# A two-block network on one core: the second mixer's modulation in runs of three pieces, two of its four vectors computed between experts and attention

## The chip, the cores and the metric

The kernel runs on one core of one Trainium2 chip. TensorE (PE) multiplies, VectorE (DVE) and ScalarE (ACT) work on whole tiles, GpSimd (POOL) and SyncE (SP) mostly issue transfers, ScalarE some too. The metric is the device time of one execution in microseconds. Times inside an execution are counted from the start of its profiled span.

## The reference

Two blocks follow one another on 256 tokens of width 1024. The first has two layers (l = 0 and 1), each a hybrid mixer and a gated feed-forward network. The second has two layers as well: a pooling mixer with 16 experts, then attention over the tokens and a context with 16 experts. The second block is modulated: six vectors of 1024 numbers for each of its layers come from a conditioning vector and scale, shift and gate what the layer does.

```python
def adaln(cvec, w_mod, b_mod):
    m = jax.nn.silu(cvec) @ w_mod + b_mod          # w_mod: 1024 x 6144
    m = m.reshape(cvec.shape[:-1] + (6, 1, D_MODEL))
    return tuple(m[..., k, :, :] for k in range(6))

for i in range(DEPTH):                              # second block
    sh1, sc1, g1, sh2, sc2, g2 = adaln(c, w_mod[i], b_mod[i])
    a_lat = modulate(x, norm1_g[i], sh1, sc1)       # rmsnorm * (1 + scale) + shift
    ...
    x = x + g1 * y_lat
    x = x + g2 * hier_moe(modulate(x, norm2_g[i], sh2, sc2), ...)
```

The vectors depend on the conditioning vector alone, so they can be computed at any time before they are used. For layer 1 of the second block they are numbered 0 to 5: shift and scale ahead of the attention (0, 1), the attention's gate (2), shift and scale ahead of the experts (3, 4), the experts' gate (5).

## The kernel before

The matmuls of the first block are exact products in three passes: a weight of 1 MB comes through `load` (line 399) on SP's queue into one of three buffers `stg`, `split` (line 413) makes a high part on ScalarE and a low part on DVE, and `prod` (line 450) issues three matmuls for each block of 128 by 128. The layers of the first block come one after the other (`mixer`, `ffn`), then the second block: `latent` (pooling and the routing of the experts), `experts0` (16 experts, four quads), `attn`, `layer1`.

The modulation is filler for the first block. `adaln` (line 1239) is a generator that is advanced by `fill` (line 597), which `pair` calls after each pair of output blocks and `ffn` between some of its steps; `finish` runs what is left. It handles the vectors that it is given, one after the other. For one vector it takes four 1 MB chunks of `w_mod`. In the first block each chunk comes as two pieces of 512 KB through `load2` (line 408), which issues on POOL's queue into one of three buffers `st2`. A piece is multiplied at line 1267 by four matmuls: 32 columns of the conditioning vectors `sc` are the weights, the piece's 256-column quarters stream, and the four results lie in four groups of 32 partitions of one PSUM bank (`ad`). After eight pieces the bank is copied to `S` (line 1279); at the next vector, four small matmuls at line 1250 turn it into columns and DVE adds the bias into `MV` (line 1251). In the second block `st2` is gone (`st2 = None`, `pools_a`): a chunk comes through `load`, its two halves are two steps of the generator, each chunk has a bank of its own, and its result is copied or added to `S` (lines 1275, 1273).

Which vectors are computed where: layer 0's six in the first mixer, layer 1's vectors 0 to 3 in the second mixer, and 4 and 5 in `latent`, right ahead of the experts.

After the experts a test of the routing's counts (`tc.If`, line 1714) stops the planner from moving instructions across it. Then `attn` (line 1883) issues eight indirect transfers on POOL (`gather`, line 1726), each of 128 rows of 4 KB that the experts wrote to DRAM. `vector_row` and `shift_rows` turn vectors 5 and 3 into rows. `combine` (line 1737) weights the gathered rows by matmuls and adds them to the tokens (`seg` 0) and the context (`seg` 1), `modulate` norms and modulates each, and the projections (`project` and what follows, weights `wqk` through `load`) begin. The list `gate` makes a load wait: one entry is taken for each call of `load`, and where it isn't None, POOL first copies a column of the gathered rows into the buffer (line 404), so the load goes out when the gathers are in. Before, the first two loads of `attn` are free and the third and fourth wait.

The order of instructions on each engine is made by a planner that simulates the program's time: it takes what is ready by the order in which the program names it. `high_priority` moves instructions ahead in that order, and `behind` (line 588) keeps one matmul after another.

Of the kernel before, what the change touches and what calls it, by code (L numbers as in the profile page):

```python
# [8 lines left out]
F32 = mybir.dt.float32  # L9
# [263 lines left out]
class Prog:  # L273
# [925 lines left out]
    def pools_m(self, ctx):  # L1199

        P = self.pools(ctx)
        self.a1 = P("a1m", 4)
        self.pmm = P("pmm3", 3, space=PSUM)
        self.pm1 = P("pm1", 1, space=PSUM)
        self.pmx = P("pmx3", 4, space=PSUM)
        self.wx = P("wx", 3)
        self.b8 = P("b8", 3)
        self.b4 = P("b4", 2)
# [30 lines left out]
    def adaln(self, l, cs):  # L1239

        nc, a = self.nc, self.a
        old = None
        for c in list(cs) + [None]:
            ps = None
            if old is not None:
                o, S = old
                ps = self.bank()
                p2 = ps[:, 256:272].rearrange("p (j n) -> p j n", j=2)
                for j in range(2):
                    nc.tensor.matmul(p2[:, j], S[:, j * 128:j * 128 + 128], self.c["s2"], start=True, stop=True)  # L1250
                nc.vector.tensor_add(self.MV[:, l, 8 * o:8 * o + 8].rearrange("p (g j) c -> p j g c", j=2),
                                     p2.rearrange("p j (g c) -> p j g c", c=2),
                                     self.v(f"bm_{l}", 8 * o, 8).rearrange("p (g j o) -> p j g o", j=2, o=1)
                                     .to_broadcast([128, 2, 4, 2]))
            if c is not None:
                S = self.as_.tile([128, 256], F32, tag="as", name="as")
                for q in range(4):
                    if self.st2 is None:
                        t = self.load(a["w_mod"][l, 4 * c + q])
                        ws = [t[:, :1024], t[:, 1024:]]  # L1260
                    else:
                        ws = [self.load2(a["w_mod"][l, 4 * c + q][:, hf * 1024:hf * 1024 + 1024]) for hf in range(2)]
                    ps = self.bank() if ps is None or self.st2 is None else ps
                    first, last = (0, 1) if self.st2 is None else (-2 * q, 7 - 2 * q)
                    for hf in range(2):
                        for n in range(4):
                            nc.tensor.matmul(ps[32 * n:32 * n + 32, :256], self.sc[:, 2 * q + hf],  # L1267
                                             ws[hf][:, n * 256:n * 256 + 256], start=hf == first, stop=hf == last)
                        if self.st2 is None and hf == 0:
                            yield  # L1270
                    if self.st2 is None:
                        if q:
                            nc.vector.tensor_add(S, S, ps[:, :256])
                        else:
                            nc.scalar.copy(S, ps[:, :256])
                    if q < 3:
                        yield
                if self.st2 is not None:
                    nc.scalar.copy(S, ps[:, :256])
                old = c, S  # L1280
            yield

    def bank(self):
        return self.pad.tile([128, 512], F32, tag="ad", name="ad")

    def mv(self, l, which, seg):
# [596 lines left out]
    def attn(self, x, xc):  # L1883
        nc, a = self.nc, self.a
        hs = []
        R = [self.R[0, 0], self.R[0, 1]]
        G = [self.gather(r) for r in R]

        self.gate += [None] * 2 + [G[1][1][:, 1, :1]] * 2
        self.vector_row(1, 5, 0)  # L1890
        for _ in self.shift_rows(1):
            pass
        for seg, xx in enumerate((x, xc)):
            self.combine(G[seg], R[seg], seg, xx)
            th, tl = self.e8(F32R), self.e8(F32R)

            def sink(kt, t, sh, th=th, tl=tl):
                nc.scalar.activation(th[:, kt], t, AF.Identity, bias=sh)
                nc.vector.scalar_tensor_tensor(tl[:, kt], t, sh, th[:, kt], op0=ALU.add, op1=ALU.subtract)
            self.modulate(xx, 1, "m1_1", 0, seg, sink)  # L1900
            hs.append([(th[:, k], tl[:, k]) for k in range(KT)])
        tabs = {"q": [self.c["cos2"], self.c["sin2"]]}
        t = self.t2()
        tabs["k"] = [t[:, 0], t[:, 1]]
# [18 lines left out]
        for m in range(2):  # L1923
            ps = self.mm()
# [220 lines left out]
    def run(self):  # L2145
        from contextlib import ExitStack
        nc = self.nc
# [7 lines left out]
        with ExitStack() as c1:  # L2155
# [5 lines left out]
            nc.sync.dma_start(x[:, 4:], xT[:, 4:])  # L2161
            nc.sync.dma_start(t[:, 1024:], self.a["w_fm"][0, 0][:, 1024:])
            self.loaded = [t]
            for l, todo in enumerate((chain([None] * 2, self.adaln(0, range(6))), self.adaln(1, range(4)))):
                self.todo = todo
                self.mixer(l, x)
                self.finish()
                if l == 0:
                    self.rows_behind()
                else:  # L2170
                    self.todo = self.context()
                self.ffn(l, x)
                self.finish()
            self.todo = self.adaln(1, range(4, 6))
        self.block2(x, hp)

    def last_stats(self, p):
# [28 lines left out]
```

## Time and profile before

| | us |
|---|---|
| median of three runs | 1724.01 (1720.69 to 1727.6) |
| the profiled execution | 1730.23 |
| its span in the profile | 1728.5 |

| engine | busy us | share of the span |
|---|---|---|
| PE (matmul) | 1650.6 | 95% |
| DVE | 1069.1 | 62% |
| ACT | 807.3 | 47% |
| POOL | 179.9 | 10% |

The page gives each engine's busy time. A busy PE may run at either of its two clock levels; the granted clock of a stretch is a share of the full one. The views used below are a table by stretch, lists of waits, and single instructions in order of time. In these, "x8" behind a group is the count of its records, and a bracket gives the idle time ahead of it and what ended that. A 32-bit matmul of the modulation stands as two records.

### The profile page before, as it was taken

To read this page: it belongs to the slowest core of one execution; us is meant where nothing else is said; L and a number is where in the kernel's file an instruction comes from. 1 tells how busy PE (TensorE), PEld (TensorE's weight loads), DVE (VectorE), ACT (ScalarE), POOL (GpSimd) and SP (SyncE) were. 2 spreads that over 40 slices of the span, in tenths; PEclk is the share of its full clock that TensorE was granted. 3 is DMA by queue.
4 is the path that set the end of the run, shared out by engine and by line. 5 is a ranking of instruction groups with operands and counts; after the bars stand their busy time and mean duration, and the time that the engine had idled before them with its cause. 6 is when DMAs were issued, how large, how long until landed. Compare 5 with 4: busy or idle time off the path is not lost. (4 is left out here: it accounts for less than half of the span.)

```text
span 1728.5 us, 29622 instructions
## 1 busy us (share of the span) xinstructions
PE 1650.6 (95%) x12089; PEld 1407.6 (81%) x12089; DVE 1069.1 (62%) x1946; ACT 807.3 (47%) x1260; POOL 179.9 (10%) x282
## 2 busy tenths in 40 slices
PE   6999999999999999999999999998999799888997
PEld 6977889999999986788999999957777598566453
DVE  5874475666665596367686777467776557555222
ACT  4542264444444373245456554436777634552121
POOL 4211001110000230101011111110000201000000
PEclk9999999999999999999999999988999889998999
DMA  8474157865555666335555648466888734118991
GB/s 332 153 254 156 57 189 252 309 243 189 179 179 187 244 192 221 123 122 208 199 184 171 204 171 270 170 244 229 323 303 302 285 126 123 31 31 316 397 402 55
DMA packets 67212, 359.73 MB, mean 208 GB/s; under 512 B 8040, under 2 KB 13080, under 8 KB 34680
## 3 DMA queue, kind: packets, MB, share of 16 engines
q1 hardware_dynamic: 41280, 279.86, 44.8%
q0 software_dynamic: 25712, 77.81, 13.3%
q8 instruction: 100, 1.64, 0.4%
q14 instruction: 48, 0.39, 0.1%
q10 hardware_dynamic: 72, 0.03, 0.0%
HBM read 339.76 MB, written 14.71 MB: 205 GB/s over the span
## 5 line engine op out<-in xcount | busy, mean ns | idle before, releaser
L424 DVE TENSOR_TENSOR wlo<-stg,whi 128x1024 fp32r<-128x1024 f32 (+1 forms) x379 | 462.3, 1226 | 298.0 <-ACT whi L421 288.2
L421 ACT ACTIVATE whi<-stg 128x1024 fp32r<-128x1024 f32 (+1 forms) x383 | 402.5, 1057 | 482.1 <-PE mm L457 287.6
L456 PE MATMUL mm<-hh,whi 128*128 128x256 f32 x1408 | 409.1, 291 | 9.5 <-ACT hh L462 9.2
L457 PE MATMUL mm<-hl,whi 128*128 128x256 f32 x1408 | 403.5, 287 | 0.7 <-DVE hl L466 0.7
L458 PE MATMUL mm<-hh,wlo 128*128 128x256 f32 x1408 | 402.9, 286 | 0.0
L456 PEld LDWEIGHTS mm<-hh,whi 128*128 128x128 f32 x1408 | 272.9, 194 | 21.6 <-ACT hh L462 9.7
L457 PEld LDWEIGHTS mm<-hl,whi 128*128 128x128 f32 x1408 | 273.0, 194 | 4.2 <-issue 2.8
L458 PEld LDWEIGHTS mm<-hh,wlo 128*128 128x128 f32 x1408 | 272.8, 194 | 2.7 <-issue 2.1
L410 POOL DMA_DIRECT2D st<-in_w_mod x80 | 42.8, 536 | 406.3 <-PE ad L1267 367.8
L493 POOL TENSOR_TENSOR a<-a,a 128x256 f32<-128x256 f32 x30 | 28.0, 935 | 313.2 <-ACT a L491 312.0
L613 PE MATMUL mm<-wlo,hh 128*128 128x512 f32 (+1 forms) x160 | 60.1, 375 | 0.0
L614 PE MATMUL mm<-whi,hl 128*128 128x512 f32 (+1 forms) x160 | 60.0, 375 | 0.0
L612 PE MATMUL mm<-whi,hh 128*128 128x512 f32 (+1 forms) x160 | 59.5, 378 | 0.0
L456 PE MATMUL mm<-lg,whi 128*128 128x256 f32 x192 | 54.5, 284 | 0.0
L456 PE MATMUL mx<-lg,whi 128*128 128x256 f32 x192 | 54.4, 285 | 0.0
L457 PE MATMUL mm<-lg,whi 128*128 128x256 f32 x192 | 54.3, 283 | 0.0
L458 PE MATMUL mm<-lg,wlo 128*128 128x256 f32 x192 | 54.3, 283 | 0.0
L1767 PE MATMUL mm<-Dt,tok 128*128 128x256 f32 x256 | 43.0, 316 | 11.8 <-ACT xg L1769 10.0
L457 PE MATMUL mx<-lg,whi 128*128 128x256 f32 x192 | 54.2, 283 | 0.0
L458 PE MATMUL mx<-lg,wlo 128*128 128x256 f32 x192 | 54.1, 283 | 0.0
L1267 PE MATMUL ad<-st,sc 128*32 128x256 f32 x640 | 52.0, 390 | 2.2 <-DMA st<-in_w_mod 2.0
L1861 DVE TENSOR_TENSOR eo<-mx,g2r 128x512 f32<-128x512 f32 x16 | 11.1, 692 | 66.1 <-PE mx L1856 65.8
(601 smaller groups left out, 3597.8 us busy)
## 6 DMA issues: line engine op xcount, KB each, us to landing
stg<-in_moe SPq DMA_DIRECT2D x57, 1024.0 KB
stg<-in_w_gu SPq DMA_DIRECT2D x44, 1024.0 KB
stg<-in_w_fm SPq DMA_DIRECT2D x43, 1024.0 KB
st<-in_w_mod POOLq DMA_DIRECT2D x80, 512.0 KB, 5.8
w<-in_moe SPq DMA_DIRECT2D x27, 1024.0 KB
stg<-in_w_dn SPq DMA_DIRECT2D x22, 1024.0 KB
stg<-in_w_tm SPq DMA_DIRECT2D x16, 1024.0 KB
stg<-in_w_br SPq DMA_DIRECT2D x12, 1024.0 KB
```

Source lines behind the costliest of these rows:

```text
L410: self.nc.gpsimd.dma_start(t, src)
L421: nc.scalar.activation(hi[:, :n], t, AF.Copy)
L424: (nc.gpsimd if pool else nc.vector).tensor_sub(lo[:, :n], t, hi[:, :n])
L456: nc.tensor.matmul(out, hi, xh, start=first and k == 0, stop=False)
L457: nc.tensor.matmul(out, hi, xl, start=False, stop=False)
L458: nc.tensor.matmul(out, lo, xh, start=False, stop=last and k == n - 1)
L493: self.adder.tensor_add(sq[0][1], sq[0][1], s)
L612: nc.tensor.matmul(ps[i], xh[:, ts], hi[:, s], start=first, stop=False)
L613: nc.tensor.matmul(ps[i], xh[:, ts], lo[:, s], start=False, stop=False)
L614: nc.tensor.matmul(ps[i], xl[:, ts], hi[:, s], start=False, stop=last)
L1267: nc.tensor.matmul(ps[32 * n:32 * n + 32, :256], self.sc[:, 2 * q + hf], ws[hf][:, n * 256:n * 256 + 256], start=hf == first, stop=hf == last)
L1767: nc.tensor.matmul(ps[:, w], tok[seg][w][:, t, k * 128:k * 128 + 128], Dt[seg][:, t].rearrange("p e s -> p (e s)"), start=t == 0, stop=t == 1)
```

## The change

In layer 1, `adaln` takes a new path while `st2` exists: `adaln_runs` loads the eight pieces of a vector in runs of three, three and two, each run a step of the generator. A run's matmuls start with its last piece, and all that follow the first are moved ahead in the planner's order (by 400) and tied one behind another. All eight pieces of a vector add up in one bank, from piece 2 (`start`) to piece 6 (`stop`).

The second mixer computes vectors 0 and 1 alone. `latent` computes 3 and 5 in place of 4 and 5. Vectors 2 and 4 are computed in `attn`: eight steps of the generator after the combine of `seg` 0, eight after that of `seg` 1, the rest before the projections. Their eight 1 MB loads go out on SP's queue ahead of the projections' weights, with no gate; the first two projection loads now wait for the gathers. Their bank is the one that the attention's output uses later (`pmo`).

```diff
--- before.py
+++ after.py
@@ -1203,6 +1203,7 @@
         self.pmm = P("pmm3", 3, space=PSUM)
         self.pm1 = P("pm1", 1, space=PSUM)
         self.pmx = P("pmx3", 4, space=PSUM)
+        self.pad = None
         self.wx = P("wx", 3)
         self.b8 = P("b8", 3)
         self.b4 = P("b4", 2)
@@ -1254,6 +1255,12 @@
                                      .to_broadcast([128, 2, 4, 2]))
             if c is not None:
                 S = self.as_.tile([128, 256], F32, tag="as", name="as")
+                if self.st2 is not None and l:
+                    ps = yield from self.adaln_runs(l, c, ps)
+                    nc.scalar.copy(S, ps[:, :256])
+                    old = c, S
+                    yield
+                    continue
                 for q in range(4):
                     if self.st2 is None:
                         t = self.load(a["w_mod"][l, 4 * c + q])
@@ -1280,7 +1287,30 @@
                 old = c, S
             yield
 
+    def adaln_runs(self, l, c, ps):
+
+        nc = self.nc
+        ps = self.bank() if ps is None else ps
+        for run in ((0, 1, 2), (3, 4, 5), (6, 7)):
+            ws = [(z, self.load2(self.a["w_mod"][l, 4 * c + z // 2][:, (z % 2) * 1024:(z % 2) * 1024 + 1024])) for z in run]
+            ms = [(z, w, n) for z, w in reversed(ws) for n in range(4)]
+
+            def mat(z, w, n):
+                return nc.tensor.matmul(ps[32 * n:32 * n + 32, :256], self.sc[:, z], w[:, n * 256:n * 256 + 256],
+                                        start=z == 2, stop=z == 6)
+            e = mat(*ms[0])
+            with self.tc.high_priority(offset=400):
+                for m in ms[1:]:
+                    f = mat(*m)
+                    self.behind(f, e)
+                    e = f
+            if run[0] != 6:
+                yield
+        return ps
+
     def bank(self):
+        if self.pad is None:
+            return self.pmo.tile([128, 512], F32, tag="su", name="ad")
         return self.pad.tile([128, 512], F32, tag="ad", name="ad")
 
     def mv(self, l, which, seg):
@@ -1886,12 +1916,15 @@
         R = [self.R[0, 0], self.R[0, 1]]
         G = [self.gather(r) for r in R]
 
-        self.gate += [None] * 2 + [G[1][1][:, 1, :1]] * 2
+        self.gate += [None] * 8 + [G[1][1][:, 1, :1]] * 2
         self.vector_row(1, 5, 0)
         for _ in self.shift_rows(1):
             pass
+        self.todo = self.adaln(1, (2, 4))
         for seg, xx in enumerate((x, xc)):
             self.combine(G[seg], R[seg], seg, xx)
+            for _ in range(8):
+                self.fill()
             th, tl = self.e8(F32R), self.e8(F32R)
 
             def sink(kt, t, sh, th=th, tl=tl):
@@ -1899,6 +1932,7 @@
                 nc.vector.scalar_tensor_tensor(tl[:, kt], t, sh, th[:, kt], op0=ALU.add, op1=ALU.subtract)
             self.modulate(xx, 1, "m1_1", 0, seg, sink)
             hs.append([(th[:, k], tl[:, k]) for k in range(KT)])
+        self.finish()
         tabs = {"q": [self.c["cos2"], self.c["sin2"]]}
         t = self.t2()
         tabs["k"] = [t[:, 0], t[:, 1]]
@@ -2161,7 +2195,7 @@
             nc.sync.dma_start(x[:, 4:], xT[:, 4:])
             nc.sync.dma_start(t[:, 1024:], self.a["w_fm"][0, 0][:, 1024:])
             self.loaded = [t]
-            for l, todo in enumerate((chain([None] * 2, self.adaln(0, range(6))), self.adaln(1, range(4)))):
+            for l, todo in enumerate((chain([None] * 2, self.adaln(0, range(6))), self.adaln(1, range(2)))):
                 self.todo = todo
                 self.mixer(l, x)
                 self.finish()
@@ -2171,7 +2205,7 @@
                     self.todo = self.context()
                 self.ffn(l, x)
                 self.finish()
-            self.todo = self.adaln(1, range(4, 6))
+            self.todo = self.adaln(1, (3, 5))
         self.block2(x, hp)
 
     def last_stats(self, p):
```

## Rows read from the trace of the kernel before

**Rows 1.** The page: busy time, share of the span, instructions of PE.

```profile
PE 1650.6 (95%) x12089; PEld 1407.6 (81%) x12089; DVE 1069.1 (62%) x1946; ACT 807.3 (47%) x1260; POOL 179.9 (10%) x282
```

**Rows 2.** Busy time by stretch, second mixer: last three clock, DMA share, GB/s.

```profile
565.00:598.00 33.00, 33.00 (x292) 29.55 (x291) 18.86 (x32) 13.54 (x21) 10.04 (x16) 1.00 0.71 254
640.00:667.00 27.00, 24.86 (x143) 15.34 (x144) 15.45 (x23) 10.58 (x17) 4.77 (x9) 1.00 0.81 286
```

**Rows 3.** Waits of PE, 515 to 815 us: total, times, longest.

```profile
PE ad L1267 <- DMA st<-in_w_mod: 2.0, 1, 2.0
```

**Rows 4.** PE in order of time, experts to attention: start, length, what.

```profile
1374.79 0.56 PE L549 MATMUL mx<-vec,MV 128*2 128x20 f32 x16
1380.36 1.20 PE L1750 MATMUL mx<-b,rows 128*128 128x128 f32 x4 [5.01 <-DMA rows<-eb,si]
...
1383.73 1.91 PE L1750 MATMUL ms<-b,rows 128*128 128x128 f32 x8
...
1389.16 1.06 PE L1750 MATMUL ms<-b,rows 128*128 128x128 f32 x8
...
1406.26 0.36 PE L457 MATMUL mm<-b,whi 128*128 128x256 f32 x1
```

**Rows 5.** Busy time by stretch, experts to attention (columns as in rows 2).

```profile
1375.00:1380.00 5.00, 0.35 (x14) 0.23 (x10) 3.16 (x5) 3.96 (x9) 3.84 (x4) 0.74 1.01 392
1380.00:1385.00 5.00, 3.48 (x14) 3.22 (x15) 2.52 (x3) 1.84 (x3) 0.94 (x1) 0.50 1.03 419
1385.00:1390.00 5.00, 5.00 (x36) 5.00 (x35) 0.00 (x0) 0.00 (x0) 0.89 (x3) 0.74 0.90 284
```

**Rows 6.** The modulation's matmuls, 515 to 815 us: records, min/median/max ns.

```profile
L1267 PE MATMUL ad<-st,sc x250: 379/379/403, 567.7 to 812.9; 128*32 128x256 f32 x125
```

**Rows 7.** PE in order of time, second mixer, around groups of the modulation.

```profile
567.71 1.05 PE L1267 MATMUL ad<-st,sc 128*32 128x256 f32 x10
...
587.45 0.28 PE L458 MATMUL mm<-hh,wlo 128*128 128x256 f32 x1
587.66 1.50 PE L1267 MATMUL ad<-st,sc 128*32 128x256 f32 x24
...
589.31 0.28 PE L457 MATMUL mm<-hl,whi 128*128 128x256 f32 x1
...
594.71 0.28 PE L457 MATMUL mm<-hl,whi 128*128 128x256 f32 x1
594.83 0.28 PE L458 MATMUL mm<-hh,wlo 128*128 128x256 f32 x1
595.04 0.64 PE L1267 MATMUL ad<-st,sc 128*32 128x256 f32 x8
...
595.83 0.28 PE L457 MATMUL mm<-hl,whi 128*128 128x256 f32 x1
...
759.48 0.51 PE L1250 MATMUL ad<-cst_cg,as 128*128 128x8 f32 x4
...
812.24 1.07 PE L1267 MATMUL ad<-st,sc 128*32 128x256 f32 x16
```

**Rows 8.** The modulation's 512 KB loads, line 410: issue to landing.

```profile
DMA to landing us min/median/max: 3.8/5.9/9.8
```

**Rows 9.** SP, POOL and ACT in order of time, experts to attention.

```profile
1367.54 21.28 SPq L405 DMA_DIRECT2D stg<-in_wqk  x4
...
1370.93 1.04 POOL L1732 DMA_INDIRECT rows<-eb,si  x1 [2.91 <-ACT a L528]
...
1379.66 1.06 ACT L421 ACTIVATE whi<-stg 128x1024 fp32r<-128x1024 f32 x1 [1.04 <-issue]
...
1388.28 0.31 POOL L404 COPY stg<-rows 128x1 f32<-128x1 f32 x2 [0.32 <-DMA rows<-eb,si]
```

**Rows 10.** DMA queues (q1 is SP's, q0 POOL's), 1371 to 1377 us: packets, MB.

```profile
q1 hardware_dynamic: 198, 1.37, 55.1%
q0 software_dynamic: 254, 0.98, 44.0%
```

## The prediction

> **What bounds the kernel now.** I read the page's busy shares first, then the stretches, then the waits, then single instructions. TensorE (PE) is busy for 95% of the span [rows 1], but that is a mean, so the two places that the change touches were read by themselves. [...]
>
> The second place is the wait between experts and attention, from 1365 to 1406 us. PE ends its row work at 1375.35, then sits idle for 5.01 us until the first gathered rows land at 1380.36; after that it works on the combine, and the attention's projections run in earnest from 1406.26 [rows 4]. [...]
>
> **The change part by part.** *Modulation left in the second mixer.* Before, it has 4 vectors there, each of 32 matmuls of a 128 by 32 weight block, which the trace counts as 64 records; the trace kept 250 of 256 [rows 6]. Eight records are a piece (512 KB), so there are 32 pieces. What a group costs is read from the starts of its neighbours, which come every 0.12 us where nothing is between them. One piece alone: from L458 at 594.83 to the second matmul after the group at 595.83 are 1.00 us, less two steps of 0.12 leaves 0.76 us [rows 7]. Three pieces in one group: 587.45 to 589.31 are 1.86, less 0.24 leaves 1.62 us [rows 7]. The difference, 0.86 for two pieces, is 0.43 us a piece, and what is left is 0.33 us for each time that PE turns to this shape and back. Reading the timeline from the first group at 567.71 to the last at 812.24 [rows 7], I count 27 groups of 2 to 24 records. Cost before: 27 x 0.33 + 32 x 0.43 = 8.9 + 13.8 = 22.7 us. After: 2 vectors, 16 pieces in 6 runs: 6 x 0.33 + 16 x 0.43 = 2.0 + 6.9 = 8.9 us. That is 13.8 us less. Each vector also has a turn-over into columns, four records of 0.51 us in all [rows 7]; two of them go, 1.0 us. Sum: **14.8 us less**, all on PE where it is full.
>
> *The wait of a run.* A run starts with its last piece, so PE now waits for three loads where it waited for one, six times in all, and every matmul of the projections queued behind it on PE waits too. Before, no run exists, so the price has bounds: below, the one old wait of 2.0 us goes too (-2.0); above, the time from issue to landing, which is 5.9 us in the middle and 9.8 at worst [rows 8], so 3.9 us for each of six runs, 23 us. I take 0, since 32 waits on these loads came to 2.0 us [rows 3] and the first run's loads can be issued long ahead. On POOL's queue a run's three loads wait together for the three buffers; behind them stand the second mixer's compression weights, which use the same buffers, and its small casts. I cost this at nothing: PE did not wait for either before [rows 3].
>
> *Two vectors moved into the wait.* They bring 8 loads of 1 MB on SP's queue, through three buffers, ahead of the first load of the projections' weights; 8 times 16 records; a copy or an add for each load on ScalarE or DVE; and the two turn-overs. PE's part at full clock is 8 x (0.33 + 2 x 0.43) + 1.0 = 10.5 us. Before, two projection loads went ahead of the gathers, and the second had landed by 1379.66, where its split starts [rows 9]. Now three buffers are filled at once, 1.05 MB more ahead of the gathers; at some 400 GB/s [rows 5] that is 2.6 us later for the first rows. Of the 10.5 us, two loads (2.4 us) fit the 5.01 us of idle time and two more (2.4) the added 2.6; **5.7 us** are left, beside the combine and, since PE is full from 1406 on, on the path. The work also keeps PE busy in the idle time. At half clock a group of eight combine matmuls takes 1.91 us, at full 1.06 [rows 4]; about four such groups run before 1387, so a clock that stays up gives back at most 3.4 us, at least 0. I take half, 1.7. Together: 2.6 + 5.7 - 1.7 = **6.6 us more**.
>
> The projections' first load is now the ninth on SP's queue and waits for the gathers (on POOL, where the gate's copy ran at 1388.28 [rows 9]). By count, 8.4 MB of modulation and 4.2 MB of gathers must have moved since 1367.5 [rows 9] before it starts: 12.6 MB, 31 us at 400 GB/s, so it would start at about 1399, land at about 1402 and be split by ScalarE in 1.06 us [rows 9]; needed at 1406, it is just in time, and I cost it at nothing. If it is late, the projections and all behind are late by as much.
>
> The two vectors that ran just before the experts are still two there (3 and 5 for 4 and 5): nothing. Sum: -14.8 + 6.6 = **-8.2 us**. The profiled execution took 1730.2 us (span 1728.5) and would take 1722.0. It is 6.2 us above the median of the runs, 1724.0, so the forecast for the median is 1715.8.
>
> [...] Rows show that loads on SP's queue took 1.37 MB and the gathers 0.98 MB of the same six microseconds, 1371 to 1377 [rows 10]. [...]
>
> **The rivals.** *The wait hides everything* (chance 0.2): loads land evenly, PE does all eight in idle time, the clock stays up. Then nothing is left but the clock's 3.4 us as a gain, and -14.8 - 3.4 = -18.2 gives **1706**. For it: idle PE time and a low clock [rows 4, 5]. Against: only three loads can be in flight, and five of eight must land after the rows begin to.
>
> *The gathers starve* (0.22): SP refills a buffer as soon as PE frees it, so the gathers stay at 0.98 MB in 6 us, 163 GB/s [rows 10]. Eight gathers of 0.52 MB, 4.19 MB, from 1371 on take 25.7 us and end at 1396.7 in place of 1388.3 [rows 9], 8.4 us later, and the combine, the norm and the gated projection loads follow. With the 5.7 us of PE work: -14.8 + 14.1 = -0.7, **1723**. For it: a full DMA [rows 5]. Against: PE may be held by other work, and then SP can't refill.
>
> *A run waits for its third piece* (0.1), the one that ends slower: three loads are issued together as the three buffers come free, beside the streamed weights, and if the last lands at 9.8 us where the order of PE reckoned with 5.9 [rows 8], PE stands for 3.9 us in each of six runs, 23.4 us: -8.2 + 23.4 = +15.2, **1739**. It is no gain from 1.4 us a run, and slower by over 0.5% from 2.8 us a run. Against: one wait of 2.0 us in 32 [rows 3].
>
> *The runs are broken up* (0.05): other matmuls get between the pieces, as now. Then half of 22.7 and the turn-overs go, 12.4 us, and with 6.6 the net is -5.8, **1718**.
>
> **How the numbers follow.** The forecast has 0.43, and spreads from 1709 to 1721, half of it on either side of -0.5%. A measurement of this kernel can tell about 0.5%, 8.6 us, from no change: below 1715.4 is faster, above 1732.6 slower. Faster: 0.2 from the first rival, 0.22 from the forecast, 0.03 from the broken runs, 0.45. Slower: 0.1 from the waiting runs, 0.03 from the starved gathers where the late projection load adds to them, 0.13. The rest, 0.42, is no change. The range takes in the hidden wait with the old 2.0 us stall gone (1704) and the starved gathers with some run waits on top of them (8 us, 1731): 1703 to 1732.
>
> **What would show it.** Right: from 515 to 815 us six groups of 16 or 24 records in place of 27, no new PE wait, and the second mixer some 15 us shorter; 128 records of the same line between 1355 and 1400 of the new trace; the projections starting about 8 us earlier than 1406 in absolute time. Wrong: PE waits on the modulation's loads at the runs' first matmul; a gather that lands over 5 us later relative to the end of the experts; or the projections' first matmul waiting for a split of its own weights.

## The result: 1.2% slower, and the profile after

The changed kernel takes 1748.4 us (median of 4 runs, 1743.2 to 1752.4) against 1724.3 before: a ratio of 1.0122, 95% interval 1.0087 to 1.0156. The forecast was 1715.8. The profiled execution took 1752.3 us against 1730.2.

Where the time went is read by comparing the start of the same PE instruction in both profiled executions (after minus before; each figure is the median of the matmuls within 6 us of the place, modulation left out). The places are times of before:

```
place (us)        565   640   667   690   715   765   815   845  1079  1210  1365  1434  1720
after - before   +6.4  +5.4  -0.8  -2.5  +5.7  +2.8 +12.2 +12.0 +12.0 +10.8  +9.6 +25.2 +23.5
```

So the second mixer, forecast to end 14.8 us earlier, ends 12.0 later, and all of that appears after 690. From there to the experts' end nothing is lost (+12.0 to +9.6). The wait before attention (1365 to 1434) adds 15.6 us where 6.6 were forecast; 13.9 of them are left at the end.

**The second mixer.** The page's first row, and PE's waits from 515 to 830 us, kernel after (beside [rows 1, 3]):

```profile
PE 1669.2 (95%) x12089; PEld 1424.7 (81%) x12089; DVE 1070.7 (61%) x1952; ACT 807.4 (46%) x1260; POOL 171.5 (10%) x266
```

```profile
PE mx L887 <- DVE a L782: 7.2, 1, 7.2
PE mm L456 <- DVE G L923: 1.0, 1, 1.0
```

PE has as many matmuls as before and is busy 18.6 us longer with them; it doesn't wait for a load any more. One new wait of 7.2 us ends at 803 us: products of the mixer's chain that PE reached before DVE had their input. A second, of 1.0 us, stands behind 815. Line numbers in the rows are those of each kernel's own file (L1299 is the modulation's matmul of a run, L1274 that of a chunk in the wait, L1780 the combine). Now the stretches. Columns are those of [rows 2]: length, busy PE, PEld (loading of PE's weights), DVE, ACT, POOL, each with its count of instructions, then granted clock, DMA share, GB/s. First before, then after:

```profile
690.00:715.00 25.00, 25.00 (x287) 19.45 (x286) 11.31 (x18) 3.95 (x5) 7.13 (x14) 1.00 0.44 152
790.00:815.00 25.00, 25.00 (x225) 23.41 (x225) 19.46 (x45) 13.35 (x21) 2.65 (x5) 1.00 0.64 230
```

```profile
640.00:667.00 27.00, 27.00 (x169) 21.07 (x167) 21.94 (x32) 16.16 (x24) 1.59 (x3) 1.00 0.63 220
690.00:715.00 25.00, 25.00 (x173) 21.15 (x173) 9.74 (x15) 3.81 (x4) 0.00 (x0) 0.73 0.22 71
790.00:815.00 25.00, 17.81 (x124) 17.24 (x123) 14.77 (x27) 13.76 (x23) 3.25 (x6) 0.80 0.45 148
```

From 640 to 667 the old wait for a load is gone: PE is busy for all 27.00 us, before for 24.86 [rows 2]. PE shows 25.00 of 25.00 us busy from 690 to 715 in both, but 173 matmuls in place of 287 and a clock of 0.73. Busy says nothing about speed here: the clock has gone to its lower level (0.50 from 697.7 to 711.4, after 1.00 from 690 to 697.6). Between 515 and 830 us the trace of after has 37.5 us at that level (13.7 from 697.7 on, then 10.2, 3.4 and 10.2), before 3.4. In PE's order of time around the first fall, the projections' matmuls start every 0.12 us before it and every 0.22 us behind it:

```profile
694.01 0.28 PE L456 MATMUL mm<-hh,whi 128*128 128x256 f32 x1
694.13 0.28 PE L457 MATMUL mm<-hl,whi 128*128 128x256 f32 x1
...
694.45 0.38 PE L1044 MATMUL mx<-lg 64*128 64x256 f32 x1
694.76 0.23 PE L1046 MATMUL mx<-aqkb,idb 128*128 128x128 bf16 x1
...
698.54 0.41 PE L457 MATMUL mm<-hl,whi 128*128 128x256 f32 x1
698.76 0.41 PE L458 MATMUL mm<-hh,wlo 128*128 128x256 f32 x1
```

Before it fell, PE alternated small products of the mixer's chain (L1044, L1046) with few projections. The modulation is over by then: its 128 records run from 508.9 to 664.7, and nothing of it lies between 690 and 815, where before had 128 records, 16 pieces (the last of them in [rows 7]). Of the six runs five stand whole and one is in ten parts:

```profile
534.46 0.62 PE L1299 MATMUL ad<-st,sc 128*32 128x256 f32 x2
535.01 0.39 PE L457 MATMUL mm<-lg,whi 128*128 128x256 f32 x1
...
576.30 1.50 PE L1299 MATMUL ad<-st,sc 128*32 128x256 f32 x24
```

**The wait before attention.** The experts' last matmul on PE ends at 1375.0 (before 1365.4). PE in order of time (beside [rows 4]):

```profile
1384.82 1.03 PE L1274 MATMUL ad<-stg,sc 128*32 128x256 f32 x13
1392.80 1.94 PE L1274 MATMUL ad<-stg,sc 128*32 128x256 f32 x16 [6.95 <-ACT a L528]
1395.35 1.94 PE L1274 MATMUL ad<-stg,sc 128*32 128x256 f32 x16 [0.61 <-DVE as L1280]
1397.21 2.08 PE L1780 MATMUL mx<-b,rows 128*128 128x128 f32 x8
...
1422.12 1.07 PE L1274 MATMUL ad<-stg,sc 128*32 128x256 f32 x16 [0.49 <-ACT as L1282]
```

ACT, SP and POOL in order of time (beside [rows 9]):

```profile
1388.29 4.05 ACTq L529 DMA_DIRECT2D rowd<-a  x2
1392.38 0.37 ACT L1282 COPY as<-ad 128x256 f32<-128x256 f32 x1 [5.34 <-DMA stg<-in_w_mod]
```

```profile
1377.15 44.87 SPq L405 DMA_DIRECT2D stg<-in_w_mod  x8
1423.50 7.50 SPq L405 DMA_DIRECT2D stg<-in_wqk  x3
```

```profile
1423.30 0.18 POOL L404 COPY stg<-rows 128x1 f32<-128x1 f32 x1 [24.99 <-PE ad L1274]
```

Each chunk needs the one accumulation bank `ad`. The first chunk's copy out of it (L1282) stood on ACT behind two small DMA issues that took 4.05 us from the start of the first to the end of the second; the idle time in its bracket holds them, as an issue doesn't count as busy. The second chunk waited 6.95 us for that copy: it starts at 1392.80, and the copy ends at 1392.75 (the bracket names L528, the next instruction on ACT). On PE's queue the combine stood behind three chunks. It begins 22.3 us after the experts' end, before 14.9. The last chunks stand late in PE's order, so the buffers came free late, the gate's copy waited for them until 1423.3, and the projections' first load left at 1423.5. The transfers had run dry by then (columns as above; the first two rows are the whole way from the experts' end to the place 1434 of the table, before and after):

```profile
1365.44:1434.00 68.56, 56.82 (x440) 54.45 (x440) 33.93 (x86) 28.77 (x63) 9.37 (x12) 0.85 0.50 183
1374.96:1459.20 84.24, 72.48 (x575) 62.75 (x576) 37.75 (x96) 30.65 (x67) 9.20 (x12) 0.80 0.66 249
...
1413.00:1419.00 6.00, 6.00 (x34) 6.00 (x34) 3.09 (x14) 0.00 (x0) 0.00 (x0) 0.59 0.00 0
```

Over the whole way PE is idle for 11.7 us before and 11.8 after: what the wait adds is busy time, 15.7 us. The gathers came late as well. The eighth and the landings of all eight (after):

```profile
1388.82 0.95 POOL L1762 DMA_INDIRECT rows<-eb,si  x1 [0.31 <-issue]
DMA to landing us min/median/max: 9.8/13.5/18.7
```

It landed at 1407.5, 32.5 us after the experts' end, where before it was in at 1388.28 [rows 9], 22.8 us after. PE has no recorded wait for a row in after.

### The profile page after: what moved, and what is told of

Read it like the earlier page. It is cut to its first block, busy times and chain, and to the rows that moved or that the text cites. A ratio compares the mean times of both kernels' runs of the same rounds, so it can differ in the third digit from the quotient of the medians.

```text
span 1750.5 us, 29622 instructions
## 1 busy us (share of the span) xinstructions
PE 1669.2 (95%) x12089; PEld 1424.7 (81%) x12089; DVE 1070.7 (61%) x1952; ACT 807.4 (46%) x1260; POOL 171.5 (10%) x266
## 3 DMA queue, kind: packets, MB, share of 16 engines
q0 software_dynamic: 23408, 69.42, 11.7%
## 5 line engine op out<-in xcount | busy, mean ns | idle before, releaser
L410 POOL DMA_DIRECT2D st<-in_w_mod x64 | 34.1, 535 | 424.2 <-PE ad L1274 206.0
L424 DVE TENSOR_TENSOR xlo<-stg,xhi 128x1024 fp32r<-128x1024 f32 x31 | 37.9, 1221 | 16.6 <-ACT xhi L421 16.4
L1797 PEld LDWEIGHTS mm<-Dt,tok 128*128 128x128 f32 x256 | 37.7, 210 | 11.0 <-ACT xg L1799 7.3
```

What stands on the lines that cost most here:

```text
L410: self.nc.gpsimd.dma_start(t, src)
L424: (nc.gpsimd if pool else nc.vector).tensor_sub(lo[:, :n], t, hi[:, :n])
L1797: nc.tensor.matmul(ps[:, w], tok[seg][w][:, t, k * 128:k * 128 + 128], Dt[seg][:, t].rearrange("p e s -> p (e s)"), start=t == 0, stop=t == 1)
```

## The experiments

Twelve kernels. Each is the kernel after with an edit, beside runs of the kernel before on the same chip (three chips; before had medians of 1726.1 beside e1 to e4, 1725.6 beside e5 to e8 and 1728.9 beside e9 to e12). The row of before has these 67 runs. "Half clock" is twice (1 minus the mean granted clock) times the span, the mean over the runs: the time that each execution spent at the lower level, taken as the 0.50 that the stretches at that level show.

```
kernel             runs  median us  ratio to before [95%]     half clock, us
before               67     -         -                              89
after                 4   1748.4    1.0122 [1.0087, 1.0156]         118
e1_runs_only         10   1729.6    0.9991 [0.9952, 1.0029]          97
e2_move_only         10   1730.4    1.0004 [0.9979, 1.0029]          93
e3_spaced            10   1731.4    1.0024 [0.9993, 1.0056]          94
e4_none_in_wait       4   1759.1    1.0162 [1.0119, 1.0205]         125
e5_empty_work         4   1755.8    1.0167 [1.0098, 1.0235]         109
e6_proj_first         4   1754.1    1.0158 [1.0106, 1.0209]         126
e7_one_bank           4   1745.7    1.0134 [1.0071, 1.0197]         127
e8_all_three          8   1737.3    1.0073 [1.0044, 1.0102]         103
e9_spaced_bank       10   1728.8    1.0002 [0.9979, 1.0024]          90
e10_move_bank        10   1726.9    1.0001 [0.9974, 1.0029]          96
e11_runs_spaced      10   1737.3    1.0035 [1.0009, 1.0061]         105
e12_one_moved        10   1729.8    0.9998 [0.9975, 1.0020]          84
```

Within one kernel, the span of an execution goes with its half clock: over 165 executions, each taken against the mean of its kernel and chip, the slope is 0.48 us of span for each us at half clock (correlation 0.87). After has 28 us more of it than before, so some 14 of its 21 us of mean span go with the clock, by this slope; the other 7 don't. The 16 executions of the four kernels whose second mixer is that of after (after, e4, e6, e7) had 108 to 144 us of it, the 67 of before 69 to 108.

**One half of the change at a time.** e1: all four vectors stay in the second mixer, in runs; nothing in the wait.

```diff
-        self.gate += [None] * 8 + [G[1][1][:, 1, :1]] * 2
+        self.gate += [None] * 2 + [G[1][1][:, 1, :1]] * 2
-        self.todo = self.adaln(1, (2, 4))
-            for _ in range(8):
-                self.fill()
-        self.finish()
-            for l, todo in enumerate((chain([None] * 2, self.adaln(0, range(6))), self.adaln(1, range(2)))):
+            for l, todo in enumerate((chain([None] * 2, self.adaln(0, range(6))), self.adaln(1, range(4)))):
-            self.todo = self.adaln(1, (3, 5))
+            self.todo = self.adaln(1, range(4, 6))
```

> The runs alone: vectors 0 to 3 stay in the second mixer, in runs of three, three and two; 4 and 5 ahead of the experts; nothing in the wait between experts and attention. Theory A (the modulation's groups in the second mixer's later half, 690 to 815 us, kept the granted clock at full speed and filled PE's waits; the changed kernel has none there, the clock is at half for 37.5 us, 697.7 to 711.4, 738.7 to 748.9, 762.6 to 766.0 and 800.1 to 810.4): twelve runs now reach further into that half, so there is less time at half clock than in the changed kernel, and the kernel takes 1718 to 1730 us. Theory B (a run that waits for its third piece is what costs): PE waits on the modulation's loads at the head of the runs, and the kernel takes over 1735 us.

1729.6 us, no change, in the band of theory A, and no wait of PE at all from 505 to 848 us: theory B falls. Runs don't make PE wait for loads. Nor do they gain what they save: the mixer ends at +2.6 us with 17.1 us at half clock.

e2: the move alone, the second mixer's pieces one by one as before.

```diff
-                if self.st2 is not None and l:
+                if False:
```

> The move alone: two vectors in the second mixer piece by piece as before, 3 and 5 ahead of the experts, 2 and 4 in the wait. Theory A: the two vectors end early in the mixer, as in the changed kernel, the clock falls after them, and the wait costs its 14 us: 1738 to 1755 us. Theory B: without runs the mixer gains its share (some 12 us), the wait costs 14: 1722 to 1732 us.

1730.4, no change; the mixer ends 7.0 us earlier (13.7 us at half clock), the wait takes 9 us back. This missed the band of theory A, 1738 to 1755, and lies in theory B's: without the runs, the move costs nothing in sum. So the loss needs both parts together.

**Spreading the runs.** e3: two empty generator steps behind each step of a run.

```diff
+def spaced(it, n):
+    for _ in it:
+        yield
+        for _ in range(n):
+            yield
-            for l, todo in enumerate((chain([None] * 2, self.adaln(0, range(6))), self.adaln(1, range(2)))):
+            for l, todo in enumerate((chain([None] * 2, self.adaln(0, range(6))), spaced(self.adaln(1, range(2)), 2))):
```

> The changed kernel with two empty steps of the generator after each of its own in the second mixer, so that the six runs spread over it and do not end by 665 us; all else as changed. Theory A: runs in the later half hold the clock there, the time at half clock falls below 15 us, and the kernel takes 1726 to 1738 us. Rival C (the later half is slow because the planner orders its chains differently, whatever the clock, and nothing fills their waits): no gain, 1743 to 1752 us.

1731.4, as theory A had it: the same matmuls, in another order, are 17 us of the median faster, and the mixer ends at -6.7 in place of +12.0. The last two runs of the second vector now stand at 751 and 761 us. A stretch of e3:

```profile
690.00:715.00 25.00, 25.00 (x262) 20.43 (x261) 12.91 (x22) 6.46 (x8) 3.97 (x8) 1.00 0.26 86
```

The clock holds from 690 to 715 although no modulation stands there, and the 7.2 us wait is gone. So the new order is at fault, and filler in every stretch isn't needed for a clock of 1.00.

e5 tests the filler by itself: fifteen steps of unused products of the modulation's shape (16 records each, no loads) behind the two vectors.

```diff
+    def idle_work(self, n):
+        for _ in range(n):
+            ps = self.bank()
+            for z in range(2):
+                for i in range(4):
+                    self.nc.tensor.matmul(ps[32 * i:32 * i + 32, :256], self.sc[:, z], self.r, start=z == 0, stop=z == 1)
+            yield
-            for l, todo in enumerate((chain([None] * 2, self.adaln(0, range(6))), self.adaln(1, range(2)))):
+            for l, todo in enumerate((chain([None] * 2, self.adaln(0, range(6))), chain(self.adaln(1, range(2)), self.idle_work(15)))):
```

> The changed kernel with added work whose result nobody reads: after the two vectors, each of the next 15 steps of the second mixer's filler issues eight matmuls (16 records) of the modulation's shape into the modulation's bank, on operands that lie in SBUF, so with no load and no split. They cost 15 x 1.2 = 18 us of PE by rows of the kernel before. Theory A (what the second mixer lost, 12 us in place of a gain, is granted clock: 37.5 us at half, and a half-clock microsecond costs 0.52 us, from two executions of one and the same PE order, 37.5 and 27.3 us at half and 5.3 us apart): the added work holds the clock, under 15 us at half clock, and the mixer ends within 4 us of the changed kernel, for all its added work; total 1742 to 1752 us. Rival C (the planner's order alone): the time at half clock stays over 25 us, the mixer ends 14 to 20 us later, total 1760 to 1770 us.

1755.8, between the two bands; 30.7 us at half clock from 515 to 830, where theory A had under 15, so the filler didn't hold the clock. The mixer ends 6.7 us later than that of after, more than theory A's 4 and less than rival C's 14 to 20. The clock fell at 697.9, the same place as in after, with 0.73 in the same stretch:

```profile
690.00:715.00 25.00, 25.00 (x161) 18.76 (x161) 9.92 (x15) 4.07 (x5) 0.00 (x0) 0.73 0.13 43
```

Its added matmuls stood from 675 to 687 and from 701 on, none in between, so it doesn't show what one there would have done.

e11 spreads four vectors (e1 with one empty step; the edit is shown against e1, `spaced` is that of e3).

```diff
-            for l, todo in enumerate((chain([None] * 2, self.adaln(0, range(6))), self.adaln(1, range(4)))):
+            for l, todo in enumerate((chain([None] * 2, self.adaln(0, range(6))), spaced(self.adaln(1, range(4)), 1))):
```

> Four vectors in runs in the second mixer, nothing in the wait, and one empty step after each run step, so that the runs spread over the stretch in which the pieces stood before. Theory A (runs save 0.33 us for each group that is no more there, and bunching costs what the clock then loses): 12 groups in place of 27 save 5 us, the clock stays up, the mixer ends 3 to 7 us earlier, the median is 1716 to 1722. Rival C (runs themselves bring the low clock, wherever they stand): over 10 us at half clock from 515 to 830 us as in the runs without empty steps, the mixer ends at -1 to +4 us, the median is 1724 to 1732.

1737.3, a ratio of 1.0035: theory A is missed. C's signs are there (13.7 us at half clock, the mixer at +1.5), its band in microseconds is not, on a chip where before took 1728.9 and not 1724. Spreading is no cure in itself; but that runs bring the low clock wherever they stand, as C has it, falls with the profile of e12 below.

**The vectors elsewhere.** e4: the mixer as after, all four other vectors ahead of the experts; `attn` is taken back as in e1.

```diff
-            self.todo = self.adaln(1, (3, 5))
+            self.todo = self.adaln(1, range(2, 6))
```

> The second mixer as changed (two vectors in runs); vectors 2 to 5 all ahead of the experts; nothing in the wait between experts and attention. It separates the two places. The second mixer should show the same 12 us more than before as the changed kernel; from the end of the experts to the projections it should take what it took before (41 us, where the changed kernel takes 57); ahead of the experts two more vectors cost 4 to 12 us. Total 1736 to 1746 us. If the mixer is as before here, the loss there hangs on something else than its own filler.

1759.1, the worst, where 1736 to 1746 were expected. The wait is back to what it was before (the projections' tenth matmul 38.5 us after the experts' end, before 42.6), but the two vectors cost 23 us ahead of the experts (+6.7 at 1079, +29.6 at 1210), of which PE stood 6.7 us for their loads; the expectation had 4 to 12. The mixer ends at +6.7, where that of after, +12.0, was expected. Up to 706 us (712 in after) the two kernels issue PE's matmuls in the same order; then some products of the mixer's chain change places for some 6 us, and the rest is the same again up to 1182. Yet the clock fell at 697.7 in after, and in e4 not before 734. A stretch of e4:

```profile
690.00:715.00 25.00, 25.00 (x260) 20.61 (x260) 13.18 (x22) 5.04 (x7) 3.95 (x8) 1.00 0.25 86
```

27.3 us at half clock in place of 37.5, and the mixer ends 5.3 us earlier: 0.52 us for each. So the order alone doesn't settle where the clock falls; one execution falls where another doesn't. The 7.2 us wait is in both, and in e6 and e7, so that one belongs to the order.

**The wait.** e7: one accumulation bank for a whole vector in place of one for each chunk.

```diff
-                    ps = self.bank() if ps is None or self.st2 is None else ps
-                    first, last = (0, 1) if self.st2 is None else (-2 * q, 7 - 2 * q)
+                    ps = self.bank() if ps is None or self.pad is not None and self.st2 is None else ps
+                    first, last = (0, 1) if self.pad is not None and self.st2 is None else (-2 * q, 7 - 2 * q)
...
-                    if self.st2 is None:
+                    if self.pad is not None and self.st2 is None:
...
-                if self.st2 is not None:
+                if self.pad is None or self.st2 is not None:
```

> The changed kernel, but in the wait between experts and attention all eight groups of a vector add up in one bank, as in the first block, so that no group waits for the copy or the add of the one ahead. Theory E (PE's wait of 6.95 us for the bank, with the combine queued behind it, and the late refill of the load buffers that follows): that wait goes, SP's loads run closer together, and the wait grows by 5 to 9 us where it grew by 15: total 1738 to 1744 us. Theory D: the projections' weights are still ninth, but their turn comes earlier as the buffers come free earlier, so the same sign, smaller: 1743 to 1748 us. If the gathers starve behind SP's loads, nothing is gained.

The wait adds 4 to 6 us where that of after adds 14 to 16, and the 6.95 us are gone, though ACT's two DMA issues took 4.26 us again. PE of e7, whose experts end at 1377.4:

```profile
1386.51 1.07 PE L1274 MATMUL ad<-stg,sc 128*32 128x256 f32 x16
...
1392.55 4.23 PE L1274 MATMUL ad<-stg,sc 128*32 128x256 f32 x26 [0.81 <-issue]
1396.70 1.69 PE L1780 MATMUL mx<-b,rows 128*128 128x128 f32 x8
```

The median, 1745.7, is just above theory E's 1738 to 1744 and in theory D's band, and by the ratios it can't be told from after: its four runs had 127 us at half clock. Theory D isn't excluded by it: the first load of the projections left 40.6 us after the experts' end, in after 48.5.

e6: two loads of the projections ahead of the modulation's, without a gate.

```diff
-        self.gate += [None] * 8 + [G[1][1][:, 1, :1]] * 2
+        self.gate += [None] * 10 + [G[1][1][:, 1, :1]] * 2
+        self.loaded = [self.load(a["wqk"][c]) for c in (1, 2)][::-1]
```

> The changed kernel with the first two loads of the projections' weights ahead of the eight modulation loads on SP's queue, and free of the gate, as before the change. Theory D (of the 15 us that the wait between experts and attention grew, 7 are the projections' weights, which come ninth on the queue and land after the tokens are ready): the projections start when the modulated tokens are ready, some 7 us earlier, total 1738 to 1745 us. Rival E (all of it is the combine, which stands on PE behind modulation groups that wait for their bank and loads): the modulation's loads are later still and hold PE's queue longer, no gain, 1746 to 1756 us.

1754.1, no gain. The projections begin earlier (tenth matmul at 51.8 us in place of 62.8), but the modulation's loads are late in turn, and PE stands for one with the combine queued behind, and then twice for gathered rows (1.77 and 0.92 us). PE of e6:

```profile
1388.66 1.94 PE L1274 MATMUL ad<-stg,sc 128*32 128x256 f32 x16 [8.88 <-DMA stg<-in_w_mod]
...
1402.28 0.71 PE L1780 MATMUL ms<-b,rows 128*128 128x128 f32 x4 [1.77 <-DMA rows<-eb,si]
```

e8 joins e3, e6 and e7.

> The changed kernel with the runs spaced out in the second mixer, the projections' first two loads first, and one bank for a vector in the wait. If the parts add up: the second mixer 7 us shorter than before, as in the spaced version, and the wait longer by 0 to 6 us: total 1718 to 1726 us, at best a little faster than before. If the wait is paid by the gathers' share of the queues whatever the order, it stays 10 us longer and the total is 1727 to 1733 us.

1737.3, a miss: the mixer gains 5.8 us, the wait loses 15, as e6's order does. So e6's edit was left out of e9, which is e3 and e7 alone.

> The changed kernel with the two edits that each worked alone: two empty generator steps after each run step in the second mixer, and one accumulation bank for a whole vector in the wait. Theory E (the loss is two separate things, a second mixer whose order of matmuls is too dense, and a wait in which loads and the one bank come late): the second mixer ends 6 to 8 us earlier than before, the wait grows by 4 to 7 us, the median is 1718 to 1727. Rival F (the wait's cost is set by the order that the planner makes of everything ahead, so the two gains don't add): the wait grows by 10 us or more, the median is 1728 to 1740.

Both mechanisms came about as theory E had them in the profiled execution (the mixer at -5.8, the wait at +4 to +6), and the time is that of before, ratio 1.0002 on a chip where before took 1728.9. The band of E, 1718 to 1727, was missed by 2 and F's, from 1728, was hit; but F's mechanism, a wait that grows by 10 or more, isn't there, and against before on its own chip the gain of e9's profile (7.7 us of span) doesn't show in ten runs. e10 is e2 with e7's edit.

> The move alone (pieces one by one in the second mixer, two vectors in the wait), with one bank for a whole vector in the wait. Theory E: the mixer ends about 7 us earlier, the wait grows by 4 to 7 us in place of 9, the median is 1719 to 1726. Rival F: the wait still grows by 9 us or more, the median is 1728 to 1735.

1726.9 (E: up to 1726), ratio 1.0001; the mixer ends at -9.2, the wait adds 5 to 6.5 us. Its profiled execution is 12.7 us shorter than that of before; ten runs don't bear that out (1717.6 to 1738.3). e12 moves one vector, with e7's one bank; three stay in the mixer, spaced by one step (the edit beside that of e7 and `spaced`).

```diff
-        self.gate += [None] * 8 + [G[1][1][:, 1, :1]] * 2
+        self.gate += [None] * 4 + [G[1][1][:, 1, :1]] * 2
-        self.todo = self.adaln(1, (2, 4))
+        self.todo = self.adaln(1, (4,))
-            for l, todo in enumerate((chain([None] * 2, self.adaln(0, range(6))), self.adaln(1, range(2)))):
+            for l, todo in enumerate((chain([None] * 2, self.adaln(0, range(6))), spaced(self.adaln(1, range(3)), 1))):
```

> Three vectors in the second mixer in runs with one empty step after each, one vector (four loads of 1 MB in place of eight) in the wait with one bank, two before the experts as ever. Theory E (what the wait costs goes by the loads that stand ahead of the projections' weights): the mixer ends 4 to 8 us earlier, the wait grows by 0 to 3 us, the median is 1716 to 1723. Rival F (any work ahead of the combine costs what two vectors cost): the wait grows by 5 us or more, the median is 1724 to 1732.

1729.8, ratio 0.9998. No half clock at all in the mixer, which ends at -7.5; but half the loads cost the wait as much, 5 us: theory E, with 0 to 3, falls here, and F's number holds. PE (the experts' end is 1355.7):

```profile
1364.92 1.07 PE L1282 MATMUL ad<-stg,sc 128*32 128x256 f32 x16 [0.21 <-issue]
...
1371.54 3.01 PE L1282 MATMUL ad<-stg,sc 128*32 128x256 f32 x20 [0.85 <-issue]
1374.48 2.08 PE L1788 MATMUL mx<-b,rows 128*128 128x128 f32 x8
```

The combine starts 18.8 us after the experts, as in e7, e9 and e10 (19.3 to 19.4), against 14.9 before: three chunks stand ahead of it in PE's order, whether four or eight are moved. That this is what the wait pays for is argued, not shown: the gathers are late here too (the seventh landed 25.7 us after the experts' end, before 21.6).

## Why the prediction was wrong, step by step

**The second mixer, 14.8 us less, all on PE where it is full.** It ended 12.0 us later, and not for a new wait alone. The clock was read at 1.00 in two stretches [rows 2] and taken as given for the whole mixer, while the same reading was used as a variable in the wait. Put together with the terms of the prediction, the profiled executions read as follows. Groups and records from 505 us to the mixer's end; 0.33 us a group, 0.43 for 8 records, 0.5 for each four turn-over records, 0.48 for each us at half clock, and PE's waits, all against before. (The trace of before kept all 256 records in 28 groups, not 250 in 27: six stand at 509 us, ahead of the window of [rows 6].)

```
kernel            groups records half clock waits | groups pieces turn clock waits  sum  measured
before                28     256        3.4   2.0 |
after                 15     128       37.5   8.2 |  -4.3   -6.9 -1.0 +16.4  +6.2 +10.4    +12.0
e1_runs_only          21     256       17.1   0.0 |  -2.3    0.0  0.0  +6.6  -2.0  +2.2     +2.6
e2_move_only          15     128       13.7   3.2 |  -4.3   -6.9 -1.0  +4.9  +1.2  -6.1     -7.0
e3_spaced             15     128        6.8   1.7 |  -4.3   -6.9 -1.0  +1.6  -0.3 -10.8     -6.7
e4_none_in_wait       15     128       27.3   8.2 |  -4.3   -6.9 -1.0 +11.5  +6.2  +5.5     +6.7
e5_empty_work         32     320       30.7   0.0 |  +1.3   +3.4 -1.0 +13.1  -2.0 +14.9    +18.7
e11_runs_spaced       19     216       13.7   0.7 |  -3.0   -2.1 -0.5  +4.9  -1.3  -2.0     +1.5
e12_one_moved         18     192        0.0   0.7 |  -3.3   -3.4 -0.5  -1.6  -1.3 -10.2     -7.5
```

The sums lie within 4.1 us of what was measured, and within 5.0 for the five kernels not listed; why the spaced ones (e3, e8, e9, e11, e12) all end 3 to 5 us above theirs isn't known. So the prices of a group and of a piece stood, and the 14.8 us came to 12.2, since one run was cut into ten parts (15 groups, not 6). What was left out was the clock, +16.4, and a wait for DVE, +6.2. That the low clock goes with the changed order is shown: the four profiled kernels with it (after, e4, e6, e7) have 27.3 to 37.5 us at half clock in the mixer, the three with the same runs spaced out (e3, e8, e9) 6.8 each. What in the order makes it fall is open: neither filler in every gap (e3 holds without it) nor more matmuls (e5) nor spreading (e11) accounts for it alone, and e4 shows that the order doesn't fix the place.

**A run's wait costs nothing.** Right: PE waited for no run in after or in e1; the old 2.0 us [rows 3] are gone as well. The rival that ended slower, 23 us of waits for a third piece, is refuted; it had the direction right, by a mechanism that isn't there. The runs broken up happened to one run of six.

**The wait, 2.6 + 5.7 - 1.7 = 6.6 us.** It was 15.6. Two terms failed. *The idle time took up nothing.* Four of the eight loads were to fit it; PE was idle as long as before (11.8 against 11.7 us), since it stood 6.95 us for the bank, which was not in the sum. So all of the moved work, 10.5 us by the prediction's prices, came on top. *The clock gave nothing back*: 0.50, 0.93, 0.64 and 0.51 in the four stretches of 6 us from 1377 to 1401, no better than [rows 5], and over the whole way to the place 1434 PE had 34 us at half clock, before 20.5, which is 6.5 us more by the slope of 0.48, where 1.7 were to come back. Together 17, against 15.6 measured. How much of it the clock is, e2 shows, which has the same edit and the same wait for the bank but 17.1 us at half clock:

```profile
1376.41 1.93 PE L1274 MATMUL ad<-stg,sc 128*32 128x256 f32 x16 [6.83 <-ACT a L528]
...
1358.74:1436.30 77.56, 64.14 (x575) 55.44 (x576) 35.87 (x94) 29.83 (x65) 9.19 (x12) 0.89 0.72 270
```

Its wait grows by 9.0; 10.5 less 1.6 for the clock, and 1.7 more of idle time, would be 10.6, so the sum is some 1.5 too high in both. With one bank for a vector (e7, e9, e10) PE is idle for 7 to 9 us and the wait adds 4 to 6.5, near the forecast, with 17.1 us at half clock in each. Between e2 and e10, equal in that, the bank is worth 2.5 us; between after and e7 the profiles differ by 9.5, most of it clock by the slope, and in the medians no gain is seen (ratios 1.0122 and 1.0134, 1.0004 and 1.0001).

The projections' first load was "just in time" at 1399 by a count of bytes, but left at 1423.5: what it waited for was a buffer, and behind that a chunk that stood late in PE's order. What that cost isn't shown: PE has no recorded wait for these weights in after, and e6, with them first, gained nothing.

The first gathered rows came no later than before (14.8 us after the experts' end, 14.9 before), where 2.6 us were forecast. But the starved gathers (second rival) did come: the last row landed 9.7 us later after the experts' end, the rival had 8.4, and over 5 was one of the prediction's own signs of being wrong. They weren't what PE waited for in after, where it reached the rows late; in e6, with one chunk ahead of the combine, it did wait for two. The gathers had 0.98 MB against SP's 1.37 before [rows 10]; after, from 1383 to 1389, packets and MB are

```profile
q1 hardware_dynamic: 238, 1.74, 69.4%
q0 software_dynamic: 194, 0.73, 29.6%
```

The gathers' packets are the smaller ones, 0.73 MB / 194 = 3.8 KB against 7.3. By count they are 194 to SP's 238, before 254 to 198 [rows 10]; what sets these shares, no run here tests.

**Nothing for the vectors ahead of the experts.** Right: from 1079 to 1365 the shift goes from +12.0 to +9.6.

**The sum.** In place of -14.8 + 6.6 = -8.2 stand +12.0 in the mixer, -2.4 from there to the experts' end and +13.9 in the wait: +23.5 at the last place of the table, 22.1 between the two profiled executions.

## What to carry to other kernels

Where PE is "full" with small products and filler, look at the granted clock and at the number of matmuls, not at the busy share, before and after: a change that takes filler out can lose to the clock what it saves, here 12.2 us saved against 16.4 lost, 0.48 us for each one at the lower level. Moved work needs more than idle time on its engine: follow its bank (PE stood 6.95 us for it here), the copy out of the bank on its engine's queue (behind two DMA issues, 4.05 us), and the buffer that the next load waits for (free at 1423.3, where the load was reckoned for 1399). And where executions of one program differ by 1% with the clock, one profile each decides nothing: e10's profile is 12.7 us shorter than that of before, and its ten runs are no faster.

## What the runs showed of the hardware

The clock fell where PE's rows show no idle time at all: 25.00 of 25.00 us busy from 690 to 715, clock 0.73. In after, the second fall came while PE ran products of 65 columns of the mixer's chain, and their pitch went from 0.13 us (ten from 737.63 to 738.89) to 0.21 (two from 738.89 to 739.32):

```profile
737.63 1.47 PE L1126 MATMUL mx<-vsw,a 128*128 128x65 f32 x10
738.89 0.64 PE L1129 MATMUL mx<-vsw,a 128*128 128x65 f32 x2
739.32 0.63 PE L1126 MATMUL mx<-vsw,a 128*128 128x65 f32 x2
```

It is not fixed by the program: after and e4, with the same order of PE's matmuls up to 706 us, had 13.7 and 0 us at half clock from 690 to 715, and the ten executions of e1 had 75 to 122 us of it in all. The price is 0.48 us of span for each us at half clock over 165 executions, and 0.52 between the profiles of after and e4.

Two DMA issues of 2 KB each on ACT's queue took, from the start of the first to the end of the second, 4.05 us in after, 4.10 in e2 and 4.26 in e7 (in after 0.23 us each, at 1388.29 and 1392.11, with nothing on ACT between them); in after and e2 a copy that PE needed stood behind them. A full DMA alone doesn't account for it: it was full then (a share of 1.01 in after from 1388.3 to 1392.3), but from 1383.9 to 1385.2, at a share of 1.00, four issues of the same kind in after started 0.27 to 0.36 us apart. The cause is open.
